# One layer of a hybrid trunk: three hi/lo splits at the end of w_up done by GpSimd, the last tile's middle taps issued between the work of the tile in front

## The chip, the core and the metric

The kernel is one program on one core of one Trainium2 chip. It is written as instruction streams for TensorE (matmuls), VectorE, ScalarE, GpSimd and SyncE (SP, which here only issues DMAs). The metric is the device time of one execution in microseconds; the time of a kernel is the median of several executions. A hardware profile of one execution gives the start, the duration and the inferred waits of each instruction; in it a helper's line stands for all its callers.

## What is computed

One transformer-like layer for 128 context tokens and 512 latent tokens (640 rows), model width 1024, all in float32: adaptive modulation, attention and a short gated convolution side by side, an output projection, and at the end the feed-forward part, where the change lies:

```
def conv_ffn(u, p):
    up = dwconv3(u @ p["w_up"], p["conv_ffn"])
    g, val = jnp.split(up, 2, axis=-1)
    return (jax.nn.silu(g) * val) @ p["w_down"]

def dwconv3(x, w):
    xp = jnp.pad(x, ((0, 0), (1, 1), (0, 0)))
    return w[0] * xp[:, :-2] + w[1] * xp[:, 1:-1] + w[2] * xp[:, 2:]
```

The hidden width is 2816, that is 22 tiles of 128 features; w_up has a gate half and a value half, so each tile is a pair of 128 columns. After w_down come a root-mean-square norm, a gate and the residual.

## The kernel before

**Splits.** A float32 operand is cut in two fp32r parts, hi = round(x) by ScalarE (an ACTIVATE with Copy) and lo = x - hi by VectorE (a TENSOR_TENSOR subtract), and a product is three matmuls: hi·hi, hi·lo, lo·hi. A split thus always is one ScalarE instruction followed by one on VectorE; the matmuls with lo wait for the second. Weights are split in pieces of 128 x 1024, activations in rows of 128 x 642 (640 tokens and two separating columns).

**Order.** TensorE, ScalarE and VectorE each execute in the order in which the code issues; within this section the code's order is a schedule written by hand. The queues of GpSimd and SP are ordered by the compiler's scheduler. Semaphores connect the engines. Every engine's queue is in order, so an instruction that waits holds all behind it.

**w_up.** Tiles j = 2 to 21 go through `strassen(j)`: seven block products (A11, A12, S2, S1, S3, S4, A22 in this order, twelve matmuls of 322 columns each), between which the other engines prepare the left operands of the next product (`hi_of` L1017, `lo_of` L1021), add up results into the two rows of C of the tile (`added` L1041, `copied` L1038, `last_copy` L1654), and work on the tile three in front (FLAG = 3): `tap_mid` (L1509, ScalarE: Y = middle tap x C), `taps_out` (L1514, VectorE: two SCALAR_TENSOR_TENSOR per half, Y = tap x C + Y, the gate half i = 0 and the value half i = 1), `silu` (L1519, ScalarE, on the gate half), `gated` (L1523, VectorE: gate x value), `act_hi` (L1529, ScalarE) and `act_lo` (L1533, VectorE), whose results ACTa and ACTb are the left operand of w_down. Y has four rows, so tiles j and j + 2 use the same two; ACTa and ACTb have four rows, one a tile.

**w_down.** Its left 512 output columns are accumulated during w_up in five PSUM banks: `down(k)` adds tile k with 15 matmuls (5 token tiles, 3 products, L157 to L159, or L1569 where `late` is set, which runs all hi·hi, then all hi·lo, then all lo·hi). Its weights are cut in place: `down_hi(q)` (L1547, ScalarE) and `down_lo(q)` (L1551, VectorE) fill the single tile WD with tiles 2q and 2q + 1, so `down_hi(q)` must wait for the last matmul that reads the pair before. The right 512 columns are done afterwards from weight units (`next_unit`: issue the DMA of the unit three ahead, cut the unit one ahead with `split`, L131 on ScalarE and L132 on VectorE). `again(i, ts)` multiplies the last four tiles of activations, k = 18 + i, with unit i // 2 for the token tiles ts.

**The end of w_up.** `strassen(21)` has no next tile to prepare; there it also cuts a weight unit and starts on tile 19 (g = 19: both `tap_mid`, `taps_out`, `silu`), finishes tile 18, runs `down(17)`, and calls `down_hi(9)` and `down_lo(9)` between the products S3 and S4. Behind it, with w, x, y = 19, 20, 21, stands the hand-written end, L1889 to L1928: for each of the three tiles taps, silu, `gated`, `act_hi`, `act_lo`, then `down`, with `again` between as work for TensorE. `down(21)` needs everything of tile 21. Then `finish` takes the five left-hand accumulators, and the steady right-hand part and the tail follow, bounded by TensorE (L1929 on).

Of the kernel before, what the change touches and what calls it, by code (L numbers as in the profile page):

```python
# [11 lines left out]
F32 = mybir.dt.float32  # L12
F32R = mybir.dt.float32r
AF = mybir.ActivationFunctionType
ALU = mybir.AluOpType
# [46 lines left out]
def trunk_layer(ctx, tc, x_prompt, x_sample, cache_k, cache_v, c, c_ctx, w_ada, b_ada, g_pre1, g_post1, g_pre2,  # L62
# [3 lines left out]
    V, S, G, PE = nc.vector, nc.scalar, nc.gpsimd, nc.tensor  # L66
# [25 lines left out]
    def nm(s):  # L92
        cnt[0] += 1
        return f"{s}_{cnt[0]}"
# [16 lines left out]
    state = {"next": 0, "raw": [], "cut": [], "limit": 10}  # L111
# [11 lines left out]
            a = k * self.n + c0  # L123
            return tuple(x[:, a:a + (self.n if cols is None else cols)] for x in self.parts)

    def split(raw):

        n = raw.shape[1]
        hi = wp.tile([128, 1024], F32R, tag="whi", name=nm("whi"), bufs=3)
        lo = wp.tile([128, 1024], F32R, tag="wlo", name=nm("wlo"), bufs=3)  # L130
        S.activation(hi[:, :n], raw, AF.Copy)  # L131
        V.tensor_tensor(out=lo[:, :n], in0=raw, in1=hi[:, :n].bitcast(F32), op=ALU.subtract)  # L132
        return hi, lo

    def fetch(i):
        while len(state["raw"]) < min(i, len(units), state["limit"]):
            w, k0, nk, c0, n = units[len(state["raw"])]
            raw = raw_tile()
            nc.sync.dma_start(raw[:, :nk * n].rearrange("p (k c) -> p k c", c=n),
                              w[k0 * 128:(k0 + nk) * 128, c0:c0 + n].rearrange("(k p) c -> p k c", p=128))  # L140
            state["raw"].append(raw)

    def cut_upto(m):
        while len(state["cut"]) < min(m, len(units), state["limit"]):
            w, k0, nk, c0, n = units[len(state["cut"])]
            raw = state["raw"][len(state["cut"])]
            state["cut"].append(Unit(split(raw[:, :nk * n]), n))

    def next_unit():
        i = state["next"]  # L150
        state["next"] += 1
        fetch(i + 3)
        cut_upto(i + 2)
        return state["cut"][i]

    def mm3(out, ah, al, bh, bl, start, stop):
# [108 lines left out]
    with tc.tile_pool(name="pro", bufs=2) as pro, tc.manual_schedule(engines={mybir.EngineType.SP}):  # L265
# [182 lines left out]
        for f in range(KT):  # L448
            g = {0: 2, 2: 3, 4: 4, 5: 5}.get(f - 1)
# [24 lines left out]
            if f + 1 < KT:  # L474
                g = {0: 1, 1: 2, 3: 3, 5: 4, 6: 5}.get(f)
# [6 lines left out]
            if f == KT - 3:  # L482
                V.tensor_scalar(out=gains[0], in0=gains[0], scalar1=HD ** -0.5, scalar2=None, op0=ALU.mult)
                for i in range(2):
                    for a in range(2):
                        V.tensor_tensor(out=tabs[i][:, :, 0, a * 32:a * 32 + 32], in0=rt[:, :, 0, a * 32:a * 32 + 32],
                                        in1=gains[i][:, :, a * 32:a * 32 + 32].broadcast_to((128, 4, 32)), op=ALU.mult)
                        for hf in range(2):
                            d0, s0 = a * 32 + hf * 16, a * 32 + (1 - hf) * 16
                            V.tensor_tensor(out=tabs[i][:, :, 1, d0:d0 + 16], in0=rt[:, :, 1, d0:d0 + 16],  # L490
                                            in1=gains[i][:, :, s0:s0 + 16].broadcast_to((128, 4, 16)), op=ALU.mult)
# [17 lines left out]
    with tc.tile_pool(name="att", bufs=2) as at:  # L509
# [352 lines left out]
        for g in range(NKV):  # L862
            if g and g + 1 < NKV:
                q_begin(g + 1)
            for i in range(0 if g else 1, 9):
# [9 lines left out]
                if i == 2:  # L875
                    hi, lo = values(g)
# [19 lines left out]
                if i in (4, 6, 8) or (i == 1 and g):  # L896
                    hi, lo = values(*((g - 1, 3) if i == 1 else (g, (i - 4) // 2)))
# [88 lines left out]
        hi, lo = values(NKV - 1, 3)  # L986
# [16 lines left out]
    def bank(i):  # L1003
        if i >= 2 and len(pools) == 1:
            early.close()
            pools.append(ctx.enter_context(tc.tile_pool(name="pb", bufs=1, space=bass.MemoryType.PSUM)))
        return pools[i >= 2].tile([128, 512], F32, tag=f"b{i}", name=nm(f"b{i}"))


    cut, raws, pair, TT = {}, {}, {}, {}  # L1010
# [293 lines left out]
    for j in range(KT):  # L1304
# [8 lines left out]
        _, hi, lo = cut["v", j]  # L1313
# [145 lines left out]
    def crows(j):  # L1459
        if "c" not in room:  # L1460
            room["c"] = region(ra, "r3", [7, NCOL], F32, "C")
        return room["c"][:, j % 4, :], room["c"][:, 4 + j % 3, :]
# [9 lines left out]
    def plain_copy(j, tok, i):  # L1472
        dst = crows(j)[i][:, tok * HALF:(tok + 1) * HALF]
        S.activation(dst, plain_out[j, tok, i], AF.Copy, scale=(1.0, -1.0)[i])
# [25 lines left out]
    def acts(j):  # L1500
        if "y" not in room:
            room["y"] = region(rb, "r7a", [4, NCOL], F32, "Y")
            room["act"] = [rb.tile([128, NRING, NACT], F32R, tag=f"r6{x}", name=f"ACT{x}") for x in "ab"]
        ys = [room["y"][:, (2 * j + i) % 4, 0:NACT] for i in range(2)]
        return ys, [x[:, j % NRING, :] for x in room["act"]]

    def tap_mid(j, i):
        y, o = acts(j)[0][i], i * NJ + j
        S.activation(y, crows(j)[i][:, 1:1 + NACT], AF.Copy, scale=cffn[:, 44 + o:45 + o])  # L1509

    def taps_out(j, i, ds=(0, 2)):
        y, o = acts(j)[0][i], i * NJ + j
        for d in ds:
            V.scalar_tensor_tensor(out=y, in0=crows(j)[i][:, d:d + NACT], scalar=cffn[:, 44 * d + o:44 * d + o + 1], in1=y,  # L1514
                                   op0=ALU.mult, op1=ALU.add)

    def silu(j):
        y = acts(j)[0][0]
        S.activation(y, y, AF.Silu)  # L1519
# [8 lines left out]
        ys, parts = acts(j)  # L1528
        S.activation(parts[0], ys[0], AF.Copy)  # L1529

    def act_lo(j):
        ys, parts = acts(j)
        V.tensor_tensor(out=parts[1], in0=ys[0], in1=parts[0].bitcast(F32), op=ALU.subtract)  # L1533


    dn = {"raw": {}, "pms": None}
# [9 lines left out]
            room["wd"] = rb.tile([128, 2, 1024], F32R, tag="r7b", name="WD")  # L1546
        S.activation(room["wd"][:, 0, :], dn["raw"][q], AF.Copy)  # L1547

    def down_lo(q):
        hi, lo = (room["wd"][:, i, :] for i in range(2))  # L1550
        V.tensor_tensor(out=lo, in0=dn["raw"][q], in1=hi.bitcast(F32), op=ALU.subtract)  # L1551

    def wd_step(pm, t, act, w, start, stop):
        c0 = 0 if t == 0 else 1 + t * 128
        mm3(pm, act[0][:, c0:c0 + 128], act[1][:, c0:c0 + 128], *w, start, stop)

    def down(k, late=False):

        if dn["pms"] is None:
            dn["pms"] = [bank(i) for i in DBANKS]  # L1560
        w = [room["wd"][:, i, (k % 2) * 512:(k % 2) * 512 + 512] for i in range(2)]
        if not late:
            for t in range(NT):
                wd_step(dn["pms"][t], t, acts(k)[1], w, k == 0, k == NJ - 1)
            return
        for n, (i, h) in enumerate(((0, 0), (0, 1), (1, 0))):
            for t in range(NT):
                c0 = 0 if t == 0 else 1 + t * 128
                PE.matmul(dn["pms"][t], acts(k)[1][i][:, c0:c0 + 128], w[h], start=False, stop=n == 2 and k == NJ - 1)  # L1569

    def strassen(j):

        f, nxt = j - FLAG, j + 1 if j + 1 < NJ else None
        g = NJ - FLAG if nxt is None else None
        cg, cv = crows(j)
        pair[j] = tuple(bank(n)[:, 0:HALF] for n in BANKS[j])
        if j > NPLAIN:
            last_copy(j - 1)
        else:
            plain_copy(1, 1, 1)  # L1580
        if f >= 0:
            tap_mid(f, 0)
        lo_of((j, 1))
        product(j, "A11")

        copied(j, "p1", 0)
        if f >= 0:
            tap_mid(f, 1)
            taps_out(f, 0, (0,))
        product(j, "A12")  # L1590

        hi_of((j, 2), left(j, 2))
        added(cg[:, 0:HALF], j, "p1", 1)
        if f >= 0:
            taps_out(f, 0, (2,))
        lo_of((j, 2))
        product(j, "S2")

        copied(j, "u2", 0)
        if f >= 0:  # L1600
            silu(f)
            taps_out(f, 1)
        product(j, "S1")

        copied(j, "p5", 1)
        hi_of((j, 3), left(j, 3))
        if f >= 0:
            gated(f)
        if nxt:
            adds = sums(nxt)  # L1610
            adds[0]()
        if g:
            cut_upto(len(state["cut"]) + 1)
            tap_mid(g, 0)
            tap_mid(g, 1)
        if j >= DLAG:
            down(j - DLAG)
        product(j, "S3")

        added(cv[:, HALF:], j, "p5", 0)  # L1620
        lo_of((j, 3))
        if nxt:
            pair_load(j + 2)
            hi_of((nxt, 0), left(nxt, 0))
            lo_of((nxt, 0))
            adds[1]()
        q = max((j - DLAG + 1) // 2, 0)
        if j == NPLAIN or (j > DLAG and (j - DLAG) % 2 == 1):
            down_hi(q)
            down_lo(q)  # L1630
            down_load(q + 2 if q else 1)
            if q == 0:
                down_load(2)
        if f >= 0:
            act_hi(f)
        if g:
            act_lo(f)
            taps_out(g, 0)
            silu(g)
        product(j, "S4")  # L1640

        if nxt:
            hi_of((nxt, 1), left(nxt, 1))
        added(cg[:, HALF:], j, "u2", 1)
        if nxt:
            adds[2]()
        if g:
            taps_out(g, 1)
        elif f >= 0:
            act_lo(f)  # L1650
        product(j, "A22")

    def last_copy(j):
        S.activation(crows(j)[1][:, 0:HALF], pair[j][0], AF.Copy)  # L1654
# [237 lines left out]
    w, x, y = NJ - 3, NJ - 2, NJ - 1  # L1892
# [7 lines left out]
    act_lo(w)  # L1900
    tap_mid(x, 1)
    taps_out(x, 0)
    silu(x)
    taps_out(x, 1)
    down(w, True)
    gated(x)
    down_hi(NJ // 2 - 1)
    act_hi(x)
    down_lo(NJ // 2 - 1)
    act_lo(x)  # L1910
    pms.append(bank(BANKS[NJ - 1][0]))
    again(0, (2,))
    next_unit()
    tap_mid(y, 0)
    tap_mid(y, 1)
    taps_out(y, 0)
    silu(y)
    again(1, range(3))
# [59 lines left out]
```

## Time and profile before

| what | us |
|---|---|
| median of 3 executions | 1133.82 |
| lowest and highest of them | 1132.58 and 1134.37 |
| the profiled execution, its own time | 1132.64 |
| its span in the profile | 1130.9 |
| start of strassen(21)'s product S3 on TensorE | 1026.11 |
| first matmul of down(18) | 1031.49 |
| first matmul of down(21) | 1050.07 |
| last matmul | 1124.34 |

The mean granted TensorE clock was 0.997 of full speed. In a row of instructions in order of time stand the start, the duration, the engine, the line, the operation, the tile written and those read, the shapes and how many were merged; in brackets, where there was any, the idle time of the engine ahead of it and what ended it. In a row by groups stand the count, the busy time, the mean duration in ns, and the idle time ahead. Engines overlap the fixed ends of their instructions, so from issue to issue an instruction takes a little less than its duration: 1.14 us for a VectorE split of 1024 columns that lasts 1.22.

### The profile page before, as it was taken

The numbers are of one execution on the slowest core, as the hardware profiler recorded it, in microseconds if no ns is written. First come the engines' busy times: TensorE is split into PE (matmuls) and PEld (weight loads), VectorE is DVE, ScalarE is ACT, GpSimd is POOL, SyncE is SP. The second block draws the span as 40 slices with busy tenths as digits, with TensorE's granted clock in tenths as the row PEclk, the third lists the DMA queues.
The fourth block names the chain that finished last, engine by engine and source line by source line (L and its number), as shares of the span: only waits on it lengthen the run. The fifth ranks groups of instructions, "written<-read, shape, count | busy, mean of one in ns | idle before, by whom it ended". The sixth has DMA issues, their size and how long they took to land.

```text
span 1130.9 us, 19510 instructions
## 1 busy us (share of the span) xinstructions
PE 1112.9 (98%) x7885; PEld 1023.0 (90%) x7885; DVE 794.7 (70%) x1272; ACT 570.0 (50%) x979; POOL 151.5 (13%) x195
## 2 busy tenths in 40 slices
PE   7999999999999999999999999999999999999997
PEld 6787888888999999999999889999999999998786
DVE  4587666664656788889645457888887778888644
ACT  4375666665234454544532256654555455555431
POOL 2056565653000000000000012000000000000001
PEclk9999999999999999999999999999999999999999
DMA  9632433333222223323332644232333233315722
GB/s 338 204 92 79 128 95 113 104 103 113 77 71 78 76 76 96 92 75 89 100 97 77 221 149 157 67 116 88 111 105 107 90 99 106 117 61 185 244 98 93
DMA packets 177304, 129.58 MB, mean 115 GB/s; under 512 B 6274, under 2 KB 159422, under 8 KB 177214
## 3 DMA queue, kind: packets, MB, share of 16 engines
q1 hardware_dynamic: 177102, 128.30, 36.4%
q8 instruction: 62, 1.02, 0.4%
q14 instruction: 28, 0.23, 0.1%
q10 hardware_dynamic: 112, 0.04, 0.0%
HBM read 116.87 MB, written 11.45 MB: 113 GB/s over the span
## 4 chain that ended last, share of the span: by engine, by line
PE 89%; DVE 3%; ACT 1%; issue 0%; POOL 0%; DVEq 0%; POOLq 0%; ACTq 0%
PE b L1030 45%; PE b L159 9%; PE b L157 9%; PE b L158 9%; PE s L789 3%; PE s L765 3%; PE s L589 3%; PE s L157 2%; PE s L158 2%; PE s L159 2%; PE s L209 1%; DVE Y L1514 1%; DVE wlo L693 0%; PE s L560 0%; PE b L1421 0%; DVE mx L727 0%
## 5 line engine op out<-in xcount | busy, mean ns | idle before, releaser
L1030 PE MATMUL b<-ZB,whi 128*128 128x322 f32 x1024 | 228.6, 310 | 0.0
L1030 PEld LDWEIGHTS b<-ZB,whi 128*128 128x128 f32 x1024 | 173.8, 189 | 1.6
L1030 PE MATMUL b<-ZB,wlo 128*128 128x322 f32 x512 | 159.4, 311 | 0.0
L1030 PE MATMUL b<-MT,whi 128*128 128x320 f32 x608 | 134.1, 308 | 0.0
L1030 PEld LDWEIGHTS b<-MT,whi 128*128 128x128 f32 x608 | 101.6, 188 | 0.0
L1030 PEld LDWEIGHTS b<-ZB,wlo 128*128 128x128 f32 x512 | 96.2, 188 | 0.0
L1030 PE MATMUL b<-MT,wlo 128*128 128x320 f32 x304 | 93.8, 308 | 0.0
L752 POOL TENSOR_TENSOR pr<-pr,sm 128x640 f32<-128x640 f32 x64 | 80.6, 1269 | 61.2 <-DVE sm L751 61.2
L1017 ACT ACTIVATE whi<-SUM 128x1024 fp32r<-128x1024 f32 x40 | 42.2, 1055 | 79.6 <-DVE SUM L1484 77.2
L1514 DVE SCALAR_TENSOR_TENSOR Y<-C,cffn,Y 128x642 f32<-128x642 f32 x88 | 77.5, 883 | 0.9
L742 ACT ACTIVATE pr<-s,mx,rq 128x640 f32<-128x640 f32 x64 | 56.7, 886 | 38.5 <-DVE mx L729 36.4
L132 DVE TENSOR_TENSOR wlo<-raw,whi 128x1024 fp32r<-128x1024 f32 (+1 forms) x33 | 36.1, 1094 | 52.5 <-ACT whi L131 52.0
L1030 PE MATMUL b<-UH,whi 128*128 128x320 f32 x228 | 70.5, 309 | 0.0
L1030 PE MATMUL b<-UL,whi 128*128 128x320 f32 x228 | 70.4, 309 | 0.0
L1030 PE MATMUL b<-UH,wlo 128*128 128x320 f32 x228 | 70.2, 308 | 0.0
L1021 DVE TENSOR_TENSOR wlo<-raw,whi 128x1024 fp32r<-128x1024 f32 (+1 forms) x51 | 50.4, 1019 | 25.2 <-ACT whi L1017 24.3
L1017 ACT ACTIVATE whi<-WB 128x1024 fp32r<-128x1024 f32 x38 | 40.1, 1056 | 54.8 <-DVE WB L1125 54.8
L157 PE MATMUL s<-whi,UH 128*128 128x256 f32 (+1 forms) x200 | 65.9, 329 | 0.5 <-ACT UH L376 0.3
L727 DVE TENSOR_REDUCE mx<-s 128x1 f32<-128x640 f32 x64 | 52.5, 820 | 17.5 <-PE s L589 17.2
L158 PE MATMUL s<-wlo,UH 128*128 128x256 f32 (+1 forms) x200 | 61.5, 308 | 2.2 <-DVE wlo L693 2.2
L1038 ACT ACTIVATE p<-b 128x322 f32<-128x322 f32 (+1 forms) x78 | 34.3, 439 | 58.2 <-PE b L1030 58.2
L159 PE MATMUL s<-whi,UL 128*128 128x256 f32 (+1 forms) x200 | 61.8, 309 | 0.2
(319 smaller groups left out, 2922.6 us busy)
## 6 DMA issues: line engine op xcount, KB each, us to landing
raw<-in_w_in_dram SPq DMA_DIRECT2D x48, 512.0 KB, 3.7
RAW<-in_w_up_dram SPq DMA_DIRECT2D x40, 512.0 KB, 3.8
raw<-in_w_ada_dram SPq DMA_DIRECT2D x32, 512.0 KB, 3.9
raw<-in_w_down_dram SPq DMA_DIRECT2D x22, 512.0 KB, 4.0
actd<-Y SPq DMA_DIRECT2D x18, 321.0 KB, 2.6
AFB<-actd SPq DMA_DIRECT2D x18, 321.0 KB, 6.9
XT<-in_w_ada_dram SPq DMA_DIRECT2D x9, 512.0 KB, 8.7
raw<-in_w_conv_out_dram SPq DMA_DIRECT2D x9, 512.0 KB, 4.0
```

Of the source, the lines that this page charges most:

```text
L132: V.tensor_tensor(out=lo[:, :n], in0=raw, in1=hi[:, :n].bitcast(F32), op=ALU.subtract)
L157: PE.matmul(out, ah, bh, start=start, stop=False)
L158: PE.matmul(out, ah, bl, start=False, stop=False)
L159: PE.matmul(out, al, bh, start=False, stop=stop)
L727: V.tensor_reduce(out=mx, in_=self.sc[h], axis=AX.X, op=ALU.max, negate=True)
L742: S.activation(pr, self.sc[h], AF.Exp, bias=mx, scale=rs, accum_out=sm)
L752: G.tensor_tensor(out=pr, in0=pr, in1=sm.broadcast_to((128, NTOK)), op=ALU.mult)
L1017: S.activation(to[0], raw, AF.Copy)
L1021: V.tensor_tensor(out=lo, in0=raw, in1=hi.bitcast(F32), op=ALU.subtract)
L1030: PE.matmul(out, p[:, ws], q[:, k, :], start=start and k == 0 and n == 0, stop=stop and k == 3 and n == 2, skip_group_check=True)
L1038: S.activation(t, pair[j][b], AF.Copy)
L1514: V.scalar_tensor_tensor(out=y, in0=crows(j)[i][:, d:d + NACT], scalar=cffn[:, 44 * d + o:44 * d + o + 1], in1=y, op0=ALU.mult, op1=ALU.add)
```

## The change

`split`, `cut_upto`, `next_unit`, `act_lo` and `down_lo` take the engine of the subtraction as an argument. Three subtractions go from VectorE to GpSimd (`nc.gpsimd`): `down_lo(9)` in the last tile's `strassen`, where g is 19; `act_lo(20)`; and the one in the first `next_unit` of the end. The two middle taps of tile 21, which stood behind that `next_unit`, are issued on ScalarE ahead of and behind `silu(20)` and `taps_out(20, 1)`. All else keeps its order.

```diff
-    def split(raw):
+    def split(raw, eng):
...
-        V.tensor_tensor(out=lo[:, :n], in0=raw, in1=hi[:, :n].bitcast(F32), op=ALU.subtract)
+        eng.tensor_tensor(out=lo[:, :n], in0=raw, in1=hi[:, :n].bitcast(F32), op=ALU.subtract)
...
-    def cut_upto(m):
+    def cut_upto(m, eng=V):
...
-            state["cut"].append(Unit(split(raw[:, :nk * n]), n))
+            state["cut"].append(Unit(split(raw[:, :nk * n], eng), n))
...
-    def next_unit():
+    def next_unit(eng=V):
...
-        cut_upto(i + 2)
+        cut_upto(i + 2, eng)
...
-    def act_lo(j):
+    def act_lo(j, eng=V):
...
-        V.tensor_tensor(out=parts[1], in0=ys[0], in1=parts[0].bitcast(F32), op=ALU.subtract)
+        eng.tensor_tensor(out=parts[1], in0=ys[0], in1=parts[0].bitcast(F32), op=ALU.subtract)
...
-    def down_lo(q):
+    def down_lo(q, eng=V):
...
-        V.tensor_tensor(out=lo, in0=dn["raw"][q], in1=hi.bitcast(F32), op=ALU.subtract)
+        eng.tensor_tensor(out=lo, in0=dn["raw"][q], in1=hi.bitcast(F32), op=ALU.subtract)
...
-            down_lo(q)
+            down_lo(q, G if g else V)
...
     taps_out(x, 0)
+    tap_mid(y, 0)
     silu(x)
     taps_out(x, 1)
+    tap_mid(y, 1)
     down(w, True)
     gated(x)
     down_hi(NJ // 2 - 1)
     act_hi(x)
     down_lo(NJ // 2 - 1)
-    act_lo(x)
+    act_lo(x, G)
     pms.append(bank(BANKS[NJ - 1][0]))
     again(0, (2,))
-    next_unit()
-    tap_mid(y, 0)
-    tap_mid(y, 1)
+    next_unit(G)
     taps_out(y, 0)
     silu(y)
     again(1, range(3))
```

## The prediction

> **What bounds the kernel now.** I read the page first, then the busy time by stretches, then the instructions of TensorE, VectorE and ScalarE in order of time from 1026 us on, where the edited lines run.
>
> ```profile
> span 1130.9 us, 19510 instructions
> PE 1112.9 (98%) x7885; PEld 1023.0 (90%) x7885; DVE 794.7 (70%) x1272; ACT 570.0 (50%) x979; POOL 151.5 (13%) x195
> ...
> POOL 2056565653000000000000012000000000000001
> ```
>
> Over the whole span TensorE is the bound, so only a place where it waits can give something back. GpSimd shows nothing between the 25th of its 40 slices and the last, so it is free at the edited place.
>
> ```profile
> 1036.00:1050.00 14.00, 12.69 (x54) 9.63 (x52) 12.24 (x14) 8.47 (x12) 0.00 (x0) 1.00 0.69 236
> ```
>
> The columns are PE, PEld, DVE, ACT, POOL. In these 14 us VectorE is busy 12.24 us: it, not TensorE, paces this stretch. TensorE's own rows show what that costs (start, duration, and in brackets idle time before it):
>
> ```profile
> 1030.01 0.31 PE L1030 MATMUL b<-ZT,wlo 128*128 128x322 f32 x1
> ...
> 1036.17 0.39 PE L159 MATMUL b<-whi,ACTb 128*128 128x512 f32 x1
> 1036.68 2.59 PE L1569 MATMUL b<-WD,ACTa 128*128 128x512 f32 x10
> ...
> 1043.05 2.50 PE L1569 MATMUL b<-WD,ACTa 128*128 128x512 f32 x10
> ...
> 1048.42 0.39 PE L159 MATMUL b<-whi,ACTb 128*128 128x512 f32 x1
> 1050.07 0.50 PE L157 MATMUL b<-WD,ACTa 128*128 128x512 f32 x1 [1.26 <-ACT ACTa L1529]
> 1050.41 0.40 PE L158 MATMUL b<-WD,ACTa 128*128 128x512 f32 x1
> 1050.94 0.50 PE L159 MATMUL b<-WD,ACTb 128*128 128x512 f32 x1
> ```
>
> Ten matmuls in 2.50 us, the last lasting about 0.40, is a step of (2.50 - 0.40) / 9 = 0.233 us. Against that step TensorE loses 1036.68 - 1036.17 - 0.23 = 0.28, then 1050.07 - 1048.42 - 0.23 = 1.42, 0.11 and 0.30 us: **2.1 us is the ceiling of any gain here**, 0.19% of the time. The large one is down(21) waiting for act_hi(21), and the last one for act_lo(21). VectorE's queue leads there:
>
> ```profile
> 1028.11 0.49 DVE L1041 TENSOR_TENSOR C<-b,p 128x322 f32<-128x322 f32 x1 [2.13 <-PE b L1030]
> 1028.52 0.68 DVE L1021 TENSOR_TENSOR wlo<-RAW,whi 128x512 fp32r<-128x512 f32 x1
> 1029.12 1.22 DVE L1551 TENSOR_TENSOR WD<-raw,WD 128x1024 fp32r<-128x1024 f32 x1
> 1030.26 0.82 DVE L1533 TENSOR_TENSOR ACTb<-Y,ACTa 128x642 fp32r<-128x642 f32 x1
> ...
> 1036.66 0.83 DVE L1533 TENSOR_TENSOR ACTb<-Y,ACTa 128x642 fp32r<-128x642 f32 x1 [0.81 <-ACT ACTa L1529]
> ...
> 1041.04 0.83 DVE L1523 TENSOR_TENSOR Y<-Y 128x642 f32<-128x642 f32 x1
> 1041.78 1.22 DVE L1551 TENSOR_TENSOR WD<-raw,WD 128x1024 fp32r<-128x1024 f32 x1
> 1042.92 0.82 DVE L1533 TENSOR_TENSOR ACTb<-Y,ACTa 128x642 fp32r<-128x642 f32 x1
> 1043.65 1.22 DVE L132 TENSOR_TENSOR wlo<-raw,whi 128x1024 fp32r<-128x1024 f32 x1
> 1044.79 3.52 DVE L1514 SCALAR_TENSOR_TENSOR Y<-C,cffn,Y 128x642 f32<-128x642 f32 x4
> 1048.42 0.83 DVE L1523 TENSOR_TENSOR Y<-Y 128x642 f32<-128x642 f32 x1
> 1050.05 0.83 DVE L1533 TENSOR_TENSOR ACTb<-Y,ACTa 128x642 fp32r<-128x642 f32 x1 [0.81 <-ACT ACTa L1529]
> ```
>
> ```profile
> 1026.31 1.06 ACT L1547 ACTIVATE WD<-raw 128x1024 fp32r<-128x1024 f32 x1
> ...
> 1041.90 0.75 ACT L1529 ACTIVATE ACTa<-Y 128x642 fp32r<-128x642 f32 x1 [0.39 <-DVE Y L1523]
> 1042.55 1.04 ACT L131 ACTIVATE whi<-raw 128x1024 fp32r<-128x1024 f32 x1
> 1043.49 1.54 ACT L1509 ACTIVATE Y<-C,cffn 128x642 f32<-128x642 f32 x2
> ...
> 1049.28 0.74 ACT L1529 ACTIVATE ACTa<-Y 128x642 fp32r<-128x642 f32 x1 [1.91 <-DVE Y L1523]
> ```
>
> The three splits that go to GpSimd are the rows at 1029.12 (down_lo(9)), 1042.92 (act_lo(20)) and 1043.65 (the weight unit). From issue to issue they hold VectorE 1.14, 0.73 and 1.14 us, 3.0 us together. If GpSimd did them for nothing, gated(21) at 1048.42 would come 3.0 us earlier and all 2.1 us of TensorE's waits would go.
>
> **The price on GpSimd.** That it is not for nothing is shown where both engines worked on SBUF, in the attention stage:
>
> ```profile
> 86.49 1.25 POOL L752 TENSOR_TENSOR pr<-pr,sm 128x640 f32<-128x640 f32 x1
> 87.71 2.23 POOL L752 TENSOR_TENSOR pr<-pr,sm 128x640 f32<-128x640 f32 x1
> ```
>
> ```profile
> 86.68 0.42 DVE L566 TENSOR_TENSOR QL<-s,QH 128x256 fp32r<-128x256 f32 x1 [0.25 <-ACT QH L563]
> 87.02 1.81 DVE L693 TENSOR_TENSOR wlo<-raw,whi 128x1024 fp32r<-128x1024 f32 x1
> 88.75 1.74 DVE L693 TENSOR_TENSOR wlo<-raw,whi 128x512 fp32r<-128x512 f32 x1
> ```
>
> The split L693 has the form of the edited ones: 1.22 us for 1024 columns in the row at 1029.12, 0.68 for 512 in the row at 1028.52. Here it took 1.81 and 1.74, and GpSimd's second multiply 2.23 in place of 1.25. The ends explain it: GpSimd to 87.74, VectorE to 88.83 (1.09 later), GpSimd to 89.94 (1.11 later), VectorE to 90.49 (0.55 later). They ran strictly in turn, in the order in which they came, each only some 0.12 us shorter than alone. L566, with one operand in PSUM, ran beside GpSimd in its 0.42 us: it takes no turn. So a split on GpSimd does not leave VectorE's path if VectorE's next instruction is of that kind; it is swapped for a longer one.
>
> How much longer, by GpSimd's own rows:
>
> ```profile
> L525 POOL TENSOR_TENSOR qf<-qf,zt 128x256 f32<-128x256 f32 x14 | 10.2, 729 | 4.1 <-PE s L589 2.3 <-DVE qf L524 1.8
> L655 POOL TENSOR_TENSOR room<-room,rk 128x256 f32<-128x256 f32 x2 | 1.2, 614 | 0.1
> ```
>
> L655 and L752 repeat one value of the second operand along the row: 0.614 us for 256 columns and 1.25 for 640, so 0.19 + 1.66 ns a column. L525 has two full operands, as the splits have: 0.729 for 256, so with the same 0.19 about 2.11 ns a column. By the first line 642 columns cost 1.25 and 1024 cost 1.89 us; by the second, 1.54 and 2.35. No row shows a subtraction with an fp32r result on GpSimd. I take 1.54 and 2.35, the row with the same kind of operands, and keep the lower pair for the range.
>
> **The change part by part**, with the turns above.
>
> *down_lo(9) on GpSimd.* It can start when down_hi(9) ends, 1026.31 + 1.06 = 1027.37, so at 1027.45, and holds until 1029.80. It fills VectorE's wait up to 1028.11; L1041 has an operand in PSUM like L566 and isn't blocked. L1021 at 1028.52 has two SBUF operands: it ends at 1029.80 + 0.55 = 1030.35, and act_lo(18) follows at 1030.27 against 1030.26 now. Saved 1.14, given back 1.14: **0.0 us** for VectorE. But L1021's result feeds the matmul at 1030.01, which now comes at about 1030.4: TensorE loses 0.4 there. Of this, 0.28 is covered by its wait at 1036.68, and the rest by the later wait. At the lower pair GpSimd ends at 1029.34 and VectorE gains 0.45. down(18) needs the split's result only after the A22 product, so it waits for nothing.
>
> *The middle taps of tile 21.* Two ACTIVATEs, 1.54 us at 1043.49, move between the work of tile 20. tap_mid(21,0) overwrites a row of Y that act_lo(19) reads, which ends at 1036.66 + 0.83, then runs in ScalarE's idle time ahead of silu(20). tap_mid(21,1) runs behind silu(20) and pushes down_hi(10) by some 0.2 us, which ends just ahead of VectorE's turn at 1041.78. **0.0 us** by itself: now the first of the two is done at about 1043.49 + 0.82 = 1044.3, ahead of the taps at 1044.79, and with the turns below the first tap finds VectorE blocked until 1044.45 anyway. Only if it is not blocked (rival a) does the move count, since it then lets the tap start at 1042.92.
>
> *act_lo(20) and the unit's split on GpSimd.* down_lo(10) stays on VectorE, 1041.78 to 1043.03 with the waits above. act_hi(20) ends at 1042.65, so GpSimd has asked before the first tap of tile 21 (L1514) is issued, and goes first: 1043.03 + 1.54 - 0.12 = 1044.45. The tap follows to 1045.20. The unit's whi is ready (1042.55 + 1.04), so GpSimd takes its next turn, to 1045.20 + 2.35 - 0.12 = 1047.43. Second tap to 1048.18, and two more at 0.87 each to 1049.92. Now the taps end at 1044.79 + 3.52 = 1048.31. **+1.6 us** on gated(21), act_hi(21) and act_lo(21), behind which down(21) waits. Queued behind the blocked tap are all later VectorE instructions; nobody else waits for them earlier. TensorE reads ACTb(20) only in the last five matmuls of down(20), about 1045.5, and the unit's wlo at about 1047: both arrive in time or inside the wait that comes anyway. The unit's raw tile is released some 2.5 us later, so the weight load queued for it on SP leaves later too, and so do the loads into the room of the C rows, which wait for the last tap; what they bring is used in the steady part and the tail.
>
> **Sum:** 0.0 + 0.0 + 1.6 = +1.6 us. The profiled execution took 1132.64 us (span 1130.9 and 1.7 around it), so 1134.2; it lies 1.2 below the median of the runs, and against the median I predict 1133.8 + 1.6 = **1135.4 us**. The rest of the program moves back by this amount unchanged.
>
> The Trainium skill, "SBUF — State Buffer", "Who interferes with whom" and "SBUF: two separate sides", says that a VectorE instruction with two SBUF inputs and a GpSimd instruction hold one shared port pair in turn, whole instructions at a time. The rows at 87.02 agree for TENSOR_TENSOR; no row shows it for L1514, which by that rule is blocked too, as in my sum.
>
> **Rivals.** (a) *The taps are not blocked.* The turns are shown for TENSOR_TENSOR; L1514 is SCALAR_TENSOR_TENSOR. If it runs beside GpSimd, the taps follow down_lo(10) at once and end at 1042.92 + 3.52 = 1046.4, act_hi(21) is ready before TensorE asks at about 1048.8, and 1.42 + 0.11 + 0.30 of waits go, less the 0.12 left from 1030: -1.7 us, 1132.1. For it: no row against. Against: it reads two SBUF operands like L693. With no turns at all it would be the ceiling, 1131.7. (b) *Cheap turns.* GpSimd at the lower pair: tile 20 comes 0.45 earlier, and from down_lo(10)'s end the two turns and four taps take 1.13 + 0.75 + 1.77 + 0.75 + 1.74 = 6.14 us against 1048.31 - 1043.03 = 5.28 now: 0.86 - 0.45 = +0.4, 1134.2. For it: L655 and L752; against: L525. (c) *The clock.* TensorE's wait before down(21) grows from 1.26 idle to about 2.7 us. After a thin stretch at the beginning the granted clock fell to half:
>
> ```profile
> 18.00:22.00 4.00, 3.72 (x13) 2.92 (x13) 1.70 (x3) 1.14 (x3) 0.00 (x0) 0.57 1.08 383
> ```
>
> ```profile
> 7.20 1.09 PE L335 MATMUL s<-ident,xn 128*128 128x128 f32 x8 [1.79 <-DVE xn L330]
> ```
>
> A mean of 0.57 over 4 us is half speed for 4 x 0.43 / 0.5 = 3.4 us, which would cost 1.7 us more: +3.3, 1137.1, slower by 0.3%. It decides from some length of wait that the trace brackets only from below: the 1.79 us ahead of 7.20 was not followed by a drop.
>
> By the Trainium skill, "TensorE: Matmul & The Clock Gate", "What's actually happening", the clock halves after an idle window of about 3.4 us; by that rule 2.7 us would not do it, and the time stays at my sum. (d) *It does nothing,* the splits landing where nobody waits: 1133.8; against it, VectorE has no idle time between 1041.78 and 1048.3.
>
> **How the numbers follow.** Forecast 0.56, (a) 0.17, (b) 0.09, (c) 0.14, (d) 0.04. A measurement of this kernel cannot tell less than 0.2% (2.27 us) from no change. The forecast passes it if each of GpSimd's two turns takes 0.33 us more than I took, fp32r results being unpriced: a third of it, 0.20, counts as slower and 0.36 as same. (a) lies just under the bound: 0.06 faster, 0.11 same. (b) and (d) are same, (c) slower. Sum: faster 0.06, same 0.60, slower 0.34. The range 1132.2 to 1137.1 takes in (a) in part, (b), (c) and (d); the forecast's own is 1134.2 to 1136.4.
>
> **What would show it.** L1551 of the last tile on GpSimd near 1027.45 lasting 2.35, and L1021 behind it stretched from 0.68 to about 1.8; the matmul at 1030.01 some 0.4 later. Near 1043 the GpSimd split and the L1514 rows in turn, two of these lasting some 2.3 and 3.1 in place of 0.88, and TensorE's wait before down(21) near 2.7 us. Taps of 0.88 beside a busy GpSimd would prove (a); a granted clock under 1.00 after 1049 (c). A GpSimd subtraction far from 2.11 ns a column makes the size wrong.

## The result, and the profile after

| | before | changed |
|---|---|---|
| median of 15 executions, us | 1132.77 | 1135.41 |
| lowest and highest | 1132.47 and 1134.48 | 1133.98 and 1136.09 |
| the profiled execution, own time | 1132.64 | 1135.93 |
| its span | 1130.9 | 1134.1 |

The ratio is 1.0018, with a 95% interval of 1.001 to 1.0025: slower, clear of 1, but by less than the 0.2% that the prediction took as the least that can be told from no change. The 15 times of the changed kernel stand in two groups: six from 1133.98 to 1134.80, nine from 1135.32 to 1136.09. The mean granted clock of the six is 0.999, of the nine 0.994 to 0.997; a mean over the whole program does not say where the clock fell.

The page of the changed kernel:

```profile
span 1134.1 us, 19512 instructions
PE 1114.9 (98%) x7885; PEld 1024.5 (90%) x7885; DVE 796.3 (70%) x1269; ACT 569.9 (50%) x979; POOL 158.9 (14%) x198
...
POOL 2056566652000000000000012000000000002001
```

GpSimd has work in the 37th slice now; nothing else on the page moves much. This trace's clock starts 0.10 us off the one of before (L1041, in front of all edits, stands at 1028.21 and stood at 1028.11), so 0.10 is taken off where the two are compared. VectorE and GpSimd in order of time (start, duration, and in brackets the idle time ahead):

```profile
1028.21 0.49 DVE L1041 TENSOR_TENSOR C<-b,p 128x322 f32<-128x322 f32 x1 [2.13 <-PE b L1030]
1028.62 1.91 DVE L1021 TENSOR_TENSOR wlo<-RAW,whi 128x512 fp32r<-128x512 f32 x1
1030.46 0.81 DVE L1533 TENSOR_TENSOR ACTb<-Y,ACTa 128x642 fp32r<-128x642 f32 x1
...
1041.97 1.22 DVE L1551 TENSOR_TENSOR WD<-raw,WD 128x1024 fp32r<-128x1024 f32 x1
1043.11 2.23 DVE L1514 SCALAR_TENSOR_TENSOR Y<-C,cffn,Y 128x642 f32<-128x642 f32 x1
1045.37 2.90 DVE L1514 SCALAR_TENSOR_TENSOR Y<-C,cffn,Y 128x642 f32<-128x642 f32 x1
...
1050.09 0.83 DVE L1523 TENSOR_TENSOR Y<-Y 128x642 f32<-128x642 f32 x1
1051.72 0.83 DVE L1533 TENSOR_TENSOR ACTb<-Y,ACTa 128x642 fp32r<-128x642 f32 x1 [0.81 <-ACT ACTa L1529]
```

```profile
1027.55 2.44 POOL L1551 TENSOR_TENSOR WD<-raw,WD 128x1024 fp32r<-128x1024 f32 x1 [330.05 <-ACT WD L1547]
1042.91 1.74 POOL L1533 TENSOR_TENSOR ACTb<-Y,ACTa 128x642 fp32r<-128x642 f32 x1 [12.93 <-ACT ACTa L1529]
1044.61 2.97 POOL L132 TENSOR_TENSOR wlo<-raw,whi 128x1024 fp32r<-128x1024 f32 x1
```

Read the ends. VectorE's L1551 ends at 1043.19; GpSimd's act_lo(20), issued before that, at 1044.65; the first tap at 1045.34; GpSimd's unit split at 1047.58; the second tap at 1048.27. Each ends its own working time behind the other's end: 1.46, 0.69, 2.24, 0.69 us. The taps' durations of 2.23 and 2.90 in place of 0.88 are waits for GpSimd, in which the profile counts VectorE as busy; no idle time gives them away. TensorE:

```profile
1030.59 0.41 PE L1030 MATMUL b<-ZT,wlo 128*128 128x322 f32 x1 [0.32 <-DVE wlo L1021]
...
1037.07 2.48 PE L1569 MATMUL b<-WD,ACTa 128*128 128x512 f32 x10
...
1047.64 0.51 PE L158 MATMUL b<-wlo,ACTa 128*128 128x512 f32 x1 [0.33 <-POOL wlo L132]
...
1049.37 0.39 PE L159 MATMUL b<-whi,ACTb 128*128 128x512 f32 x1
1051.74 0.50 PE L157 MATMUL b<-WD,ACTa 128*128 128x512 f32 x1 [1.98 <-ACT ACTa L1529]
1052.08 0.40 PE L158 MATMUL b<-WD,ACTa 128*128 128x512 f32 x1
1052.60 0.71 PE L159 MATMUL b<-WD,ACTb 128*128 128x512 f32 x1
1053.11 0.63 PE L157 MATMUL b<-WD,ACTa 128*128 128x512 f32 x1
```

down(21) starts at 1051.74 - 0.10 = 1051.64 against 1050.07: +1.57 us. Then something else: a matmul of 512 columns lasts 0.63 us in place of 0.40. Stretches of the changed kernel, and the one of before that matches the second (PE, PEld, DVE, ACT, POOL busy, granted clock, DMA share):

```profile
1049.00:1057.00 8.00, 5.89 (x18) 4.12 (x17) 6.23 (x11) 4.79 (x11) 0.00 (x0) 0.79 0.75 278
...
1053.00:1055.00 2.00, 2.00 (x6) 1.54 (x6) 1.65 (x3) 1.06 (x3) 0.00 (x0) 0.50 0.99 387
1055.00:1057.00 2.00, 2.00 (x8) 1.60 (x7) 1.65 (x4) 2.00 (x6) 0.00 (x0) 0.72 1.01 391
1057.00:1060.00 3.00, 3.00 (x14) 2.38 (x14) 2.55 (x7) 1.30 (x6) 0.00 (x0) 1.00 0.98 330
```

```profile
1053.00:1055.00 2.00, 2.00 (x11) 1.62 (x10) 2.00 (x4) 2.00 (x5) 0.00 (x0) 1.00 1.01 385
```

The granted clock is 0.50 in this profiled execution right behind the wait, and back at 1.00 in the stretch 1057 to 1060. The mean of 0.79 over 1049 to 1057 makes 8 x 0.21 / 0.5 = 3.4 us of half speed. The row of the last matmul starts at 1127.47 - 0.10 = 1127.37 against 1124.18, +3.19 us (the 1124.34 in the table of before is its entry in the profile's chain, not the start of its row): 1.57 from VectorE's chain, and 1.62 from the clock. By their times the six executions at a mean clock of 0.999 have the first part alone (1133.98 against 1132.47, the lowest of each: +1.5) and the nine have both; one of the nine has a trace, and none of the six.

### The profile page after: what moved, and what is told of

Read it like the earlier page. It is cut to its first block, busy times and chain, and to the rows that moved or that the text cites. A ratio compares the mean times of both kernels' runs of the same rounds, so it can differ in the third digit from the quotient of the medians.

```text
span 1134.1 us, 19512 instructions
## 1 busy us (share of the span) xinstructions
PE 1114.9 (98%) x7885; PEld 1024.5 (90%) x7885; DVE 796.3 (70%) x1269; ACT 569.9 (50%) x979; POOL 158.9 (14%) x198
## 4 chain that ended last, share of the span: by engine, by line
PE 89%; DVE 3%; ACT 1%; POOL 0%; issue 0%; DVEq 0%; POOLq 0%; ACTq 0%
PE b L1030 45%; PE b L159 9%; PE b L157 9%; PE b L158 9%; PE s L789 3%; PE s L765 3%; PE s L589 3%; PE s L157 2%; PE s L159 2%; PE s L158 2%; PE s L209 1%; DVE Y L1514 1%; DVE wlo L693 0%; PE s L560 0%; PE b L1421 0%; DVE mx L727 0%
## 5 line engine op out<-in xcount | busy, mean ns | idle before, releaser
L1514 DVE SCALAR_TENSOR_TENSOR Y<-C,cffn,Y 128x642 f32<-128x642 f32 x88 | 80.8, 920 | 0.9
L132 DVE TENSOR_TENSOR wlo<-raw,whi 128x1024 fp32r<-128x1024 f32 (+1 forms) x32 | 34.9, 1090 | 52.3 <-ACT whi L131 51.8
L1021 DVE TENSOR_TENSOR wlo<-raw,whi 128x1024 fp32r<-128x1024 f32 (+1 forms) x51 | 50.4, 1019 | 25.2 <-ACT whi L1017 24.3
L1017 ACT ACTIVATE whi<-WB 128x1024 fp32r<-128x1024 f32 x38 | 40.1, 1056 | 54.8 <-DVE WB L1125 54.8
L157 PE MATMUL s<-whi,UH 128*128 128x256 f32 (+1 forms) x200 | 65.8, 329 | 0.5 <-ACT UH L376 0.4
```

Source lines behind the costliest of these rows:

```text
L132: eng.tensor_tensor(out=lo[:, :n], in0=raw, in1=hi[:, :n].bitcast(F32), op=ALU.subtract)
L157: PE.matmul(out, ah, bh, start=start, stop=False)
L1017: S.activation(to[0], raw, AF.Copy)
L1021: V.tensor_tensor(out=lo, in0=raw, in1=hi.bitcast(F32), op=ALU.subtract)
```

## The experiments

Times are medians of so many executions; the last column counts executions 1.2 us or more above the lowest of the same kernel. All edits are shown against the kernel before, that of fill against the changed kernel.

| kernel | median (n) | lowest | ratio, 95% interval | far above |
|---|---|---|---|---|
| before, beside the first four | 1132.63 (28) | 1132.33 | | 4 of 28 |
| taps_only | 1132.69 (11) | 1132.58 | 1.0000, 0.9991 to 1.0009 | 1 of 11 |
| pool_only | 1135.93 (6) | 1134.39 | 1.0029, 1.0017 to 1.0042 | 5 of 6 |
| act20 | 1134.87 (11) | 1133.27 | 1.0019, 1.0010 to 1.0028 | 9 of 11 |
| unit1 | 1135.25 (11) | 1133.65 | 1.0017, 1.0008 to 1.0026 | 7 of 11 |
| before, beside the next four | 1132.71 (33) | 1132.42 | | 8 of 33 |
| down9 | 1132.64 (11) | 1132.38 | 0.9999, 0.9990 to 1.0008 | 2 of 11 |
| fill | 1134.21 (11) | 1134.00 | 1.0013, 1.0004 to 1.0022 | 2 of 11 |
| early | 1132.15 (11) | 1131.93 | 0.9996, 0.9987 to 1.0004 | 2 of 11 |
| early2 | 1130.49 (11) | 1130.14 | 0.9981, 0.9972 to 0.9989 | 3 of 11 |
| before, beside the last two | 1132.73 (21) | 1132.32 | | 8 of 21 |
| gap2 | 1134.11 (11) | 1132.35 | 1.0011, 1.0001 to 1.0021 | 8 of 11 |
| gap34 | 1134.71 (11) | 1134.03 | 1.0010, 1.0001 to 1.0019 | see text |

The effects are near the spread of the times, so the verdicts on VectorE's chain rest on the start of gated(21), L1523, in the trace, beside 1048.42 in the kernel before and with the traces' zeros matched at a row in front of the edits. That row is the first matmul of S3 (1026.11 before); against it the traces run late by 0.09 us in unit1, 0.19 in gap34 and 1.12 in early, and early by 0.02 in taps_only and early2, 0.09 in pool_only, 0.01 in act20, 0.03 in down9, 0.10 in fill and 0.29 in gap2.

A time far above is not the half clock by itself. The profiled execution of early is counted as far above (1133.29), but its granted clock is 1.00 from 1049 to 1057, and most of its delay is there from the start: its first matmul of L157 stands at 19.28, where that of the kernel before stands at 18.29.

**taps_only: the move of the middle taps alone.**

```diff
     taps_out(x, 0)
+    tap_mid(y, 0)
     silu(x)
     taps_out(x, 1)
+    tap_mid(y, 1)
...
     next_unit()
-    tap_mid(y, 0)
-    tap_mid(y, 1)
```

> Only the move of tile 21's two middle taps; all splits on VectorE. Theory of turns: the move is worth nothing by itself, since in the kernel before the first tap row (L1514 at 1044.79) starts when VectorE is free, not when the middle tap is done: 0.0 us, between -0.2 and +0.2, no TensorE wait of another length. Rival (the move itself costs, because it delays down_hi(10) and with it down_lo(10)): +0.2 to +1.6 us, with an idle VectorE ahead of down_lo(10).

```profile
1048.40 0.83 DVE L1523 TENSOR_TENSOR Y<-Y 128x642 f32<-128x642 f32 x1
```

gated(21) starts where it did (within 0.01 us), and so does down(21). By itself the move is worth nothing.

**pool_only: the three splits on GpSimd, the middle taps left.**

```diff
-            down_lo(q)
+            down_lo(q, G if g else V)
...
-    act_lo(x)
+    act_lo(x, G)
...
-    next_unit()
+    next_unit(G)
     tap_mid(y, 0)
```

> The three splits on GpSimd, the middle taps where they were. Theory of turns: the first L1514 of tile 21 is blocked by act_lo(20) on GpSimd until about 1044.6 in any case, and the middle tap is done by about 1044.4: the same as the changed kernel within 0.2 us, that is +1.6 us over the kernel before, and 3.3 where the granted clock falls to half behind the wait. Rival (the cost is the new order of ScalarE's work): near 0 or a gain.

```profile
1044.35 5.81 DVE L1514 SCALAR_TENSOR_TENSOR Y<-C,cffn,Y 128x642 f32<-128x642 f32 x4 [1.35 <-ACT Y L1509]
...
1050.26 0.83 DVE L1523 TENSOR_TENSOR Y<-Y 128x642 f32<-128x642 f32 x1
```

```profile
1042.72 1.74 POOL L1533 TENSOR_TENSOR ACTb<-Y,ACTa 128x642 fp32r<-128x642 f32 x1 [12.92 <-ACT ACTa L1529]
1044.42 2.42 POOL L132 TENSOR_TENSOR wlo<-raw,whi 128x1024 fp32r<-128x1024 f32 x1
```

gated(21) is 1.93 us late with the zeros matched, not 1.6: 0.36 more than in the changed kernel, where at most 0.2 was expected. The first tap came 1.35 us later than VectorE was free, behind its middle tap on ScalarE, and lost its turn: GpSimd's second split ran straight behind its first, 2.42 us with no wait in it, and the four taps followed. So under turns the move of the middle taps is worth 0.36 us after all: with it a tap fits between the two splits. That the order of ScalarE's work is the cost is ruled out; the splits alone cost more than the whole change.

**act20 and unit1: one split on GpSimd each.**

```diff
# act20
-    act_lo(x)
+    act_lo(x, G)
# unit1
-    next_unit()
+    next_unit(G)
```

> Only act_lo(20) on GpSimd. Theory of turns, with the changed kernel's rows: GpSimd ends 1.46 us behind down_lo(10), the unit's split L132 on VectorE ends 1.09 behind that, the four taps follow: they end at about 1049.0 against 1048.31, +0.7 us on down(21); L132 lasts about 2.5 in place of 1.22. Rival (no turns, the split is off VectorE's path): -0.7 us, L132 lasts 1.22 beside a busy GpSimd.

> Only the weight unit's split on GpSimd. Theory of turns: GpSimd gets its turn when act_lo(20) ends on VectorE, about 1043.75, and holds 2.24 us; the first tap ends 0.69 later at 1046.7, three more at 0.87: 1049.3 against 1048.31, +1.0 us. Rival (no turns): -1.1 us, taps of 0.88 each beside a busy GpSimd.

```profile
1043.61 1.92 DVE L132 TENSOR_TENSOR wlo<-raw,whi 128x1024 fp32r<-128x1024 f32 x1 [0.62 <-ACT whi L131]
1045.46 3.52 DVE L1514 SCALAR_TENSOR_TENSOR Y<-C,cffn,Y 128x642 f32<-128x642 f32 x4
1049.08 0.83 DVE L1523 TENSOR_TENSOR Y<-Y 128x642 f32<-128x642 f32 x1
```

```profile
1043.02 0.82 DVE L1533 TENSOR_TENSOR ACTb<-Y,ACTa 128x642 fp32r<-128x642 f32 x1
1044.44 5.06 DVE L1514 SCALAR_TENSOR_TENSOR Y<-C,cffn,Y 128x642 f32<-128x642 f32 x4 [0.61 <-ACT Y L1509]
1049.61 0.83 DVE L1523 TENSOR_TENSOR Y<-Y 128x642 f32<-128x642 f32 x1
```

act20 puts gated(21) back by 0.67 us, unit1 by 1.10: 0.7 and 1.0 were expected, the rival wanted gains of 0.7 and 1.1. Taking either of these splits off VectorE makes VectorE's chain longer. One number of the expectations was off: L132 in act20 lasted 1.92, not 2.5, since it was issued 0.6 us later, when its whi was ready; it ends at 1045.53, 1.08 behind the end of act_lo(20) on GpSimd, where 1.09 was expected. Both kernels have most of their times in an upper group, though the TensorE wait ahead of down(21) grew only to 1.93 and 2.35 us, and the traces show the clock falling there. The stretch behind the wait, in act20 and in unit1:

```profile
1049.00:1057.00 8.00, 6.13 (x19) 4.57 (x20) 6.35 (x10) 5.82 (x13) 0.00 (x0) 0.79 0.88 325
1049.00:1057.00 8.00, 5.61 (x16) 4.21 (x17) 6.18 (x10) 5.14 (x11) 0.00 (x0) 0.79 0.83 295
```

**down9: only the split beside the A22 product.**

```diff
-            down_lo(q)
+            down_lo(q, G if g else V)
```

> Only down_lo(9) on GpSimd. Theory of turns: it runs from 1027.5 to 1029.9 while VectorE first waits and then stands blocked at L1021, so act_lo(18) starts within 0.1 us of the kernel before; TensorE waits 0.3 us at the A22 product, which its later wait takes up: +0.1 us in all, between -0.1 and +0.3. Rival (no turns): act_lo(18) 1.1 us earlier and -1.1 us.

```profile
1027.42 2.44 POOL L1551 TENSOR_TENSOR WD<-raw,WD 128x1024 fp32r<-128x1024 f32 x1 [330.01 <-ACT WD L1547]
```

```profile
1028.49 1.91 DVE L1021 TENSOR_TENSOR wlo<-RAW,whi 128x512 fp32r<-128x512 f32 x1
1030.33 0.82 DVE L1533 TENSOR_TENSOR ACTb<-Y,ACTa 128x642 fp32r<-128x642 f32 x1
...
1048.49 0.83 DVE L1523 TENSOR_TENSOR Y<-Y 128x642 f32<-128x642 f32 x1
```

gated(21) +0.10 us, the median as before: L1021 stood blocked for about what down_lo(9) would have taken. The TensorE wait at A22 came (0.32 us, at 1030.46), and the wait ahead of down(21) took it up: 1.17 us in place of 1.26.

**fill: TensorE kept at work through its wait.**

```diff
     again(2, range(3))
+    again(2, range(3))
```

> The changed kernel with the nine matmuls of again(2) issued twice, so that TensorE works through most of its wait ahead of down(21); tile 20's share of the right-hand output columns is then added twice for three token tiles. VectorE's chain is untouched. Theory (the half clock is set off by the wait itself): no half clock behind 1050 in any run, +1.6 us over the kernel before in every run (about 1134.1), none at 1135.9. Rival (the half clock comes from something else, as the loads or the stretch of slower execution): the same two groups of times as the changed kernel, about 1134.1 and 1135.9.

```profile
1051.54 0.50 PE L157 MATMUL b<-WD,ACTa 128*128 128x512 f32 x1
```

```profile
1049.00:1057.00 8.00, 7.87 (x34) 5.89 (x33) 6.97 (x11) 5.75 (x13) 0.00 (x0) 1.00 0.79 288
```

The start of down(21) is as late as in the changed kernel, but no wait stands in front of it, and nine of eleven executions lie within 0.33 us of 1134.00, with the clock at 0.999. The granted clock stays at 1.00 there, and the row of the last matmul starts 1.56 us later than in the kernel before, not 3.19: of the changed kernel's delay the chain's part is left, and the clock's part is gone. Two executions are far above, at a mean clock of 0.994; so "every run" was too much. It is about the rate that the kernel before shows too (20 of 82 in its three sets), and where the clock fell in those two no trace shows. A group of nine in fifteen, as in the changed kernel, is not there.

**gap2 and gap34: the wait without GpSimd.** From the kernel before:

```diff
# gap2
-    again(2, range(3))
+    again(2, range(2))
# gap34
-    again(2, range(3))
```

> The kernel before, all on VectorE, with three of the nine matmuls of again(2) left out (tile 20's share of the right-hand columns for one token tile): TensorE's wait ahead of down(21) grows from 1.26 to about 1.95 us, as long as in the changed kernel, while VectorE's chain and so the start of down(21) stay. Theory (the wait itself sets off the half clock, GpSimd has no part in it): two groups of times, about 1132.6 and about 1134.3, the second in half of the executions or more. Rival (GpSimd or the stretched VectorE instructions set it off): the spread of the kernel before, about 1132.6 in five of six.

> The kernel before without again(2) altogether (tile 20's share of the right-hand columns for three token tiles left out): a wait of about 3.35 us, down(21) starting as before. Theory: the half clock in nearly every execution, about 1134.3; the length of the wait raises the share. Rival: about 1132.6 as before.

```profile
1049.78 0.51 PE L157 MATMUL b<-WD,ACTa 128*128 128x512 f32 x1 [1.94 <-ACT ACTa L1529]
```

```profile
1050.26 0.50 PE L157 MATMUL b<-WD,ACTa 128*128 128x512 f32 x1 [3.28 <-ACT ACTa L1529]
1051.00:1053.00 2.00, 1.88 (x5) 1.50 (x6) 1.72 (x3) 0.84 (x3) 0.00 (x0) 0.56 0.95 354
```

VectorE's chain and the start of down(21) are those of the kernel before, TensorE has less to do, and both are slower, by 0.1% with an interval just clear of 1. gap34, with a wait of 3.28 us, has all eleven executions at 1134.03 or more, 1.7 above the lowest of the kernel before, and its trace shows the clock falling behind the wait. gap2, with 1.94 us, has two at about 1132.35, one at 1133.17 and eight at 1133.57 or more, not the two groups that were expected. Four of the eight lie above 1136, more than one half-speed stretch explains, and none of the eight has a trace: the profiled execution is the lowest, 1132.35, and behind its wait the clock stays at 1.00. gap34 has no work on GpSimd here and its trace shows the half clock all the same, and fill has GpSimd's work but no wait and its trace does not: so the wait itself sets the half clock off. It does not do so every time, as gap2's trace shows.

**early and early2: VectorE's chain shortened without GpSimd.** early, in strassen(21):

```diff
             cut_upto(len(state["cut"]) + 1)
+            act_hi(f)
+            act_lo(f)
             tap_mid(g, 0)
             tap_mid(g, 1)
+            taps_out(g, 0)
...
-        if f >= 0:
+        if f >= 0 and not g:
             act_hi(f)
         if g:
-            act_lo(f)
-            taps_out(g, 0)
             silu(g)
```

early2 adds, in the hand-written end, this order in place of the old one:

```
    taps_out(x, 0)
    tap_mid(y, 0)
    silu(x)
    taps_out(x, 1)
    tap_mid(y, 1)
    down(w, True)
    gated(x)
    act_hi(x)
    taps_out(y, 0)
    down_hi(NJ // 2 - 1)
    act_lo(x)
    down_lo(NJ // 2 - 1)
    silu(y)
    pms.append(bank(BANKS[NJ - 1][0]))
    again(0, (2,))
    taps_out(y, 1)
    next_unit()
    again(1, range(3))
    down(x, True)
```

> The kernel before with, inside strassen(21), act_hi(18), act_lo(18) and taps_out(19, 0) ahead of the products S3 and S4, in VectorE's idle 2.1 us ahead of 1028.1; nothing on GpSimd. VectorE reaches gated(19) 2.3 us earlier. But down_lo(10) stands in VectorE's queue ahead of tile 21's taps and must wait for down_hi(10), which waits for the last matmul of down(19), about 1041.2: only 0.5 us arrive at down(21). Theory (VectorE's queue paces, and down_lo(10) is what it meets next): -0.5 us, VectorE idle about 1.6 us ahead of L1551 near 1041. Rival (pacing ends at once): -2.0 us.

> The same, and in the hand-written end act_hi(20) ahead of down_hi(10), tile 21's middle taps as in the changed kernel, its gate taps ahead of act_lo(20) and down_lo(10), and the unit's split behind its value taps; nothing on GpSimd. Theory: act_hi(21) ends at about 1047.6, before TensorE is done with its other work at 1048.4, so all 2.1 us of waits between 1036 and 1051 go: -2.1 us, about 1130.7, and no half clock there. Rival (something else paces the end, as the loads of the steady part): less than 1 us.

```profile
1039.94 0.83 DVE L1523 TENSOR_TENSOR Y<-Y 128x642 f32<-128x642 f32 x1
1042.41 1.23 DVE L1551 TENSOR_TENSOR WD<-raw,WD 128x1024 fp32r<-128x1024 f32 x1 [1.65 <-ACT WD L1547]
```

```profile
1036.00:1050.00 14.00, 14.00 (x62) 11.25 (x61) 12.70 (x16) 7.89 (x12) 0.00 (x0) 1.00 0.75 254
```

The first two rows are early's, the stretch is early2's. early's trace runs 1.12 us late, so its gated(20) stands at 1038.82 beside 1041.04, 2.2 us earlier, and its gated(21), at 1049.06 in the trace, is 0.48 us earlier. early gains 0.56 us by the medians (its interval reaches to no change) and shows the expected idle time of 1.65 us ahead of L1551, ended by ScalarE's WD: most of the 2.2 us won in front is lost at the one split that has to wait for TensorE. early2 gives VectorE other work ahead of that split. TensorE is then busy for all of the 14.00 us in which it was busy for 12.69, with no wait between 1026 and 1056, and the kernel takes 0.9981 of the time before (0.9972 to 0.9989): -2.2 us against 2.1 expected. It beats both kernels.

## Why the prediction held, point by point

- **The ceiling of 2.1 us from TensorE's waits** stands: early2 removed them all and gained 2.2, which the spread of the times does not tell from 2.1.
- **Turns between VectorE and GpSimd.** Shown in the changed kernel for SCALAR_TENSOR_TENSOR too, which the trace of before had left open. Rival (a) falls: no tap ran at 0.88 us beside a working GpSimd. L1041, with one operand in PSUM, lasted 0.49 us beside down_lo(9) as it did without, so it took no turn, as the prediction had put it.
- **GpSimd's price.** 2.35 and 1.54 us were taken from L525. down_lo(9) took 2.44 with nothing in its way; act_lo(20) ended 1.46 us behind L1551 where 1.42 was put, the unit's split 2.24 behind the tap where 2.23 was put. Rival (b), the cheap price, falls: the times lie within 0.1 us of the estimates for two full operands, in which nothing was added for the fp32r result.
- **down_lo(9): 0.0.** act_lo(18) started at 1030.46 - 0.10 = 1030.36, not 1030.27; down9 shows the +0.10 us of the whole.
- **The middle taps: 0.0.** Right for the move alone (taps_only). The side remark that the first tap would be blocked until 1044.45 in any case missed that without the move it comes too late for its turn: pool_only, 0.36 us.
- **act_lo(20) and the unit: +1.6.** Measured 1.57 on down(21). The order of the turns was the forecast one, and the two stretched taps lasted 2.23 and 2.90 us where some 2.3 and 3.1 were named.
- **TensorE's wait: 2.7 us forecast, 1.98 measured.** The unit's wlo was said to arrive in time or inside the wait; it held the second matmul of again(2) up by 0.33 us idle (1047.64), 0.5 from start to start, and the next by 0.1, and of the delay at A22 0.24 us was left there, not 0.12. So that part of the wait came earlier.
- **The clock, rival (c).** This was mis-sized: it got a chance of 0.14 and a price of 1.7 us. The price was right (1.62 in the profiled execution), but by the times it came in nine of fifteen executions. It and the sum are not alternatives but add up, in most executions. Leaning on the length of the wait was the failing step: the trace of before bracketed the point only from below, at 1.79 us, in a stretch of other matmuls, and the forecast treated 2.7 us as probably harmless, where 1.98 us was followed by the half clock. Nor does one length decide: act20's trace has the half clock behind 1.93 us, and gap2's has none behind 1.94. The row of 0.57 at 18 to 22 us that the prediction read is a matter of chance as well: it is in the traces of before and of the changed kernel, and the other ten kernels, with the same work there, have 1.00.

So it is luck that 1135.4 us came out almost to the digit. Against the fifteen executions of the kernel before the median moved by 2.64 us, where 1.6 was forecast. The base was put at 1133.8, the median of three executions, where fifteen gave 1132.77, 1.0 lower; the half clock, left out of the sum, put about as much back into the median.

The Trainium skill, "TensorE: Matmul & The Clock Gate", "What's actually happening", gives an idle window of about 3.4 us as the condition of the half clock. The half-speed stretch does last 3.4 us here, but the traces of act20, the changed kernel, unit1 and pool_only show it behind waits of 1.93, 1.98, 2.35 and 2.91 us. So a shorter wait than that can be followed by the half clock; the measurement decides.

## What to carry to other kernels

In this kernel an elementwise split moved from VectorE to GpSimd was off VectorE's path only while VectorE had no instruction with two SBUF operands to run (TENSOR_TENSOR and SCALAR_TENSOR_TENSOR were seen); otherwise nearly its whole GpSimd time, twice VectorE's, was added in front of the next one, and the profile booked that as VectorE's busy time, so compare durations of the same form. Before buying time on a third engine, look for idle time of the pacing engine a few microseconds ahead and for an instruction in its queue that waits on another engine: moving work across those two won 2.2 us here. A TensorE wait that grew by 0.7 us cost another 1.6 us through the granted clock in some executions, and the kernel's times then fell in two groups, so that a median of three could lie in either.

## What the runs showed of the hardware that was not expected

- The half clock came to 3.4 us behind a wait of 1.98 us. Five profiled executions have it, with the same mean of 0.79 over 1049 to 1057: act20 (1.93 us idle ahead of down(21)), changed (1.98), unit1 (2.35), pool_only (2.91) and gap34 (3.28). The other seven have 1.00 there: gap2 behind 1.94 us, and six kernels with 1.26 us or less.
- By the times alone, far above the lowest are 20 of 82 at 1.26 us idle (before), about as many as with no wait there (2 of 11 in fill, 3 of 11 in early2). They are 9 of 11 at 1.93 (act20), 8 of 11 at 1.94 (gap2), 9 of 15 at 1.98 (changed), 7 of 11 at 2.35 (unit1), 5 of 6 at 2.91 (pool_only), and all 11 at 3.28 (gap34, counted from the lowest of the kernel before). So the share is higher from 1.93 us on; that it grows steadily with the wait is not shown. What decides in which executions of one kernel it comes is not known.
- A blocked VectorE instruction is not delayed by its whole length: a tap ended 0.69 us behind GpSimd's end, where one alone lasts 0.88. That its start-up had been done while it stood would explain this, but no run tests it.
- Turns go by arrival only roughly. In pool_only a tap issued at 1044.35 and a GpSimd split issued at 1044.42, both while GpSimd was still at work, went in the other order; how long ahead of its turn an instruction must stand was not tried.
